# Grouped-query attention, one core: a new order table, first K and Q pieces through SyncE, idle matmuls in the first period

## The chip, the cores and the metric

The kernel runs on one core of a Trainium2 chip. The time is the device time of one execution in microseconds (us); the number that counts is the median of several executions. The engines of the core work on instruction queues of their own: PE (TensorE, matrix multiply, with PEld for the loading of weights), DVE (VectorE), ACT (ScalarE), POOL (GpSimd) and SP (SyncE, which here only issues DMA). They wait for one another through semaphores, and each takes its instructions strictly in the order in which the program puts them.

## The reference

Batch 8, 512 positions, 32 query heads, 8 key/value heads, 64 channels; four query heads share one key/value head.

```python
scores = np.einsum('bhqd,bhkd->bhqk', Q, K_expanded) * scale      # scale = 1/8
weights = np.exp(scores - np.max(scores, axis=-1, keepdims=True))
weights = weights / (np.sum(weights, axis=-1, keepdims=True) + 1e-10)
output = np.einsum('bhqk,bhkd->bhqd', weights, V_expanded)
```

Inputs and output are fp32, with the layout (batch, position, head, channel).

## The kernel before

**Tiles.** The work is cut into pairs of query heads (128 pairs: 8 batches x 16). A pair has four score tiles, one for each block kc of 128 keys: keys on the partitions, two heads x 512 queries along the row, 128x1024 in all. `scores` (L228) fills one with two matmuls of 64 channels, one on each half of the array. The exponential turns the tile into `pt` (fp16), and `pv` (L287) multiplies it by V; V carries a column of ones, so the row sums come out beside the products. `pv` works in chunks: a chunk is one tile and one head, four matmuls (one for each block qc of queries), and a pair has eight chunks. `inverse` (L306) takes the reciprocal of the sums, `norm` (L316) scales the products into `o_sb`, and every fourth pair a 1 MB `store` (L360) goes out through SP. The kernel takes no maximum; it checks at the end that nothing has overflowed and would otherwise run `general_path`.

**Two ways to the exponential.** Of the 32 tiles of eight pairs (a period; there are 16), 27 go to ACT (`exp_act`, L245) and 5 to DVE and POOL. Which 5 is said by `DVE_KCS` (L38): one tuple for each pair of the period, with the kc that DVE takes. Such a tile is scored (D), turned into fp16 bits by DVE (U, L257), its low bits are taken (F, L262), POOL forms a slope and a product (G, L267; W, L275), and DVE adds it to the bits (P, L279). In the first period, tiles of the first two pairs go to ACT all the same, and those of the next two have G and W on DVE too.

**PSUM.** Score tiles for ACT have two buffers (`s_ps`). One region `d_ps` ("a" in the table) and one region `pv` ("b") serve in turn the sums of a pair, a DVE score tile, and the transposes of Q; each is free for its next user when DVE has read it.

**The order.** The order of all instructions is written out by hand in a table: `STEPS` (L39) for each period and `FINISH` (L50) for the last. A token is a letter and a number. S6 refills the score tile for the seventh ACT tile, A6 is its activation; V5.4-6 are chunks 4 and 5 of pair 5 (an a, b or s behind chunk 0 names the region); R and N are inverse and norm; D, U, F, G, W, P are as above, numbered by the DVE tile; T2 transposes the Q of a half unit (four pairs are a unit, half of them g = 0 or 1) on PE, C2 copies it to SBUF on DVE; H reads the check of V; B is a check of the sums; Q0 and Q1 issue on POOL the loads of Q for two periods later and of K (even periods) or V (odd periods) of the next batch. "@1" is work of the period before, "@-1" of the period after. The loop at L501 goes through the periods and skips tokens whose period does not exist, so period 0 has no @1 work.

**K.** For batches 1 to 7, `dma_k` (L175), called at S2 of odd periods, makes the transposed keys by four DMA transposes through SP and two copies, which put the other head of a couple on the other half of the partitions. For batch 0 PE transposes them (`first_k`, L163): once for the couple as it is, once swapped.

**The start.** POOL issues the loads of the first K piece and three Q pieces (with a cast from fp32 to bf16 on the way), builds the identity for the transposes, and goes on with V and the rest. PE does eight idle matmuls on zeros (L496), then transposes K (12 instructions) and the first quarter of Q (L499, L190), DVE copies each, and the first scores follow.

The steps of a period before, in part:

```python
"A0 F4@1 S1 N4@1 V5.4-6@1 G4@1 V5.6-8@1 A1 R5@1 S2 N5@1 D0b W4@1 A2 S3 U0 T1a A3 S4 "
"V6.0-1b@1 H1 V6.1-2@1 C1 V6.2-3@1 A4 P4@1 S5 D1a A5 S6 U1 V6.3-6@1 Q0 V6.6-7@1 Q1 A6 S7 "
```

Of the kernel before, what the change touches and what calls it, by code (L numbers as in the profile page):

```python
# [11 lines left out]
FP32 = mybir.dt.float32  # L12
# [22 lines left out]
VV_HI = 1.0e30  # L35


DVE_KCS = ((), (3,), (), (3,), (3,), (), (3,), (3,))  # L38
STEPS = (  # L39
# [9 lines left out]
).split()  # L49
FINISH = (  # L50
# [10 lines left out]
).split()  # L61


# [19 lines left out]
def fast_path(ctx, tc, Q, K, V, out, flag):  # L83
    nc = tc.nc
# [66 lines left out]
    def d_tile():  # L151
        return d_pool.tile([128, 2, S], FP32, name="d_ps")
# [7 lines left out]
    def region(tok):  # L160
        return {"a": d_tile, "b": pv_tile, "s": s_tile}[tok[-1]]()

    def first_k(gp, swap, bank):  # L163
        half_bank = bank.bitcast(BF16)[:, 0:S]
        ps = half_bank.rearrange("p (sc c) -> p sc c", sc=SC)
        h = 2 * gp
# [6 lines left out]
        return lambda: nc.vector.tensor_copy(out=kt_first[:, gp, swap, :], in_=half_bank)  # L173

    def dma_k(b):  # L175
        kt[b] = kt_pool.tile([128, 2, GP, S], BF16, name="kt")
# [36 lines left out]
    def by_pool(n, k):  # L213
        return n * PPAIR + ON_DVE[k][0] >= UPAIR

    pts, osb, invs, chain, sums, reads, filled, done = ({} for _ in range(8))

    def pt_of(p):
        j = p // NPAIR
# [8 lines left out]
    def scores(p, kc, ps):  # L228
        u, b, gp, g, i = place(p)
        keys = kt_first[:, gp, :, :] if b == 0 else kt[b][:, :, gp, :]  # L230
        for m in range(2):
            nc.tensor.matmul(  # L232
                ps[:, m, :],
                keys[64 * m:64 * m + 64, g ^ m, kc * 128:(kc + 1) * 128],
                qt[u][64 * m:64 * m + 64, g, i, :],
                start=True,
                stop=True,
            )
# [153 lines left out]
    def transposes(j, bank):  # L392
        u, g = divmod(j, 2)
        b, gp = divmod(u, GP)
        todo = reads[j] = []
        if u > 0:
            todo.append(trans_q(u, g, bank[:, 0, :]))
        if b == 0 and gp > 0 and g == 0:
            for swap in range(2):
                todo.append(first_k(gp, swap, bank[:, 1, swap * S // 2:]))  # L400
        if u == NU - 1 and g == 0:
            todo.append(check_v(u, bank[:, 1, S // 2:]))
# [7 lines left out]
    def step(tok, n):  # L410
# [6 lines left out]
        elif what == "A":  # L417
# [3 lines left out]
            if ON_ACT[k + 1:k + 2] == [] or ON_ACT[k + 1][0] != q:  # L421
                for d, (dq, dkc) in enumerate(ON_DVE):
                    if dq == q and not on_dve(n, d):
                        fill(p, dkc)
                        exp_act(p, dkc)
            if n == 0 and k in (0, 2):
                lo, hi, g = ((1, NPAIR, 0), (0, NPAIR, 1))[k // 2]
                trans_q(0, g, d_tile()[:, 0, :], lo, hi)()
            if (n, k) == (0, 4):
                second_loads()  # L430
        elif what in "VRN":
# [6 lines left out]
        elif what in "TCH":  # L438
            j = n * PPAIR // NPAIR + k
            if j < 2:  # L440
                pass
            elif what == "T":
                transposes(j, region(tok))
            else:
                read(j if what == "C" else (j, "v"))
        elif what == "Q":
# [28 lines left out]
                elif what == "P":  # L475
                    exp_join(p, kc)

    load_k(0, 0, 2)
    load_q(0, (0, 2, 4, 8))
    make_identity(nc, ident)  # L480
    nc.gpsimd.memset(ones, 1.0)
    nc.gpsimd.memset(off, 0)
    for j in range(2):
# [7 lines left out]
        load_v(0, gp, gp + 1)  # L491

    nc.vector.memset(warm, 0.0)
    bank = d_tile()
    for j in range(8):
        nc.tensor.matmul(bank[:, 1, :], warm[:, 0:128], warm, start=True, stop=True)  # L496
# [12 lines left out]
def general_path(tc, Q, K, V, out):  # L509
# [114 lines left out]
```

## Time and profile before

| | us |
|---|---|
| median of 3 runs | 420.08 |
| lowest, highest | 419.29, 420.71 |
| the profiled execution | 419.56 |
| its span, first to last instruction | 417.8 |
| busy: ACT, PE, DVE, POOL | 400.3, 384.4, 327.3, 274.4 |
| mean granted clock of PE | 0.978 |
| share of ACT in the chain that ended last | 77% |

The profile is that of one execution. Busy time is the time in which an engine had an instruction under way. The chain that ended last is followed backwards from the last instruction, at each step to whatever released it. Where a timeline merges instructions of one kind, it gives the start of the first, their common length, and how many they are.

### The profile page before, as it was taken

Reading aid. Unit: us, or ns where it says so; the run is one execution under the profiler, and the core shown is the slowest. Engines: PE = TensorE matmul, PEld = TensorE weight load, DVE = VectorE, ACT = ScalarE, POOL = GpSimd, SP = SyncE. Lnnn points to the kernel's source line nnn. Section 1 sums busy time; section 2 is a strip of 40 time slices with the busy share of each in tenths; the row PEclk is TensorE's granted clock in tenths of the full one; section 3 lists DMA queues with packets and bytes.
Section 4 is the critical chain, followed back from the end, with each engine's and each line's share of the span. In section 5 each row is a group of like instructions: output and inputs, shape, how many; then the busy total and the mean of one; then the engine's idle time right before and its main releaser. Section 6 shows DMA issues by size and latency. Waiting matters only on the chain.

```text
span 417.8 us, 13274 instructions
## 1 busy us (share of the span) xinstructions
PE 384.4 (92%) x5817; PEld 240.1 (57%) x5817; DVE 327.3 (78%) x621; ACT 400.3 (96%) x435; POOL 274.4 (66%) x208
## 2 busy tenths in 40 slices
PE   6899899999999999999999999999999999999995
PEld 2355556556556565655656566655655656556563
DVE  1268888797887869888797887879788787978976
ACT  2889999999999999999999999999999999999994
POOL 8316677677676767767676776767667676766660
PEclk9579999999999999999999999999999999999999
DMA  9983996849765895839939489676976599421126
GB/s 101 195 157 122 151 186 153 203 141 174 224 124 150 165 189 205 150 144 176 236 115 235 130 142 195 162 195 141 164 251 117 140 174 204 179 104 56 48 102 207
DMA packets 64078, 66.95 MB, mean 160 GB/s; under 512 B 35088, under 2 KB 38672, under 8 KB 64016
## 3 DMA queue, kind: packets, MB, share of 16 engines
q0 software_dynamic: 29184, 25.17, 41.5%
q1 hardware_dynamic: 34832, 40.90, 33.6%
q8 instruction: 46, 0.75, 0.8%
q14 instruction: 16, 0.13, 0.1%
HBM read 50.33 MB, written 33.55 MB: 201 GB/s over the span
## 4 chain that ended last, share of the span: by engine, by line
ACT 77%; PE 17%; DVE 3%; issue 1%; POOL 1%; ACTq 0%; POOLq 0%
ACT pt L246 77%; PE s_ps L232 9%; PE pv L295 5%; PE d_ps L295 1%; PE d_ps L190 1%; DVE o_sb L322 1%; DVE qt L193 1%; DVE kt_first L173 0%; POOL q_nat L146 0%; PE pv L190 0%; PE d_ps L232 0%; ACTq L246 0%; DVE u L257 0%; PE s_ps L295 0%; POOL k_nat L129 0%
## 5 line engine op out<-in xcount | busy, mean ns | idle before, releaser
L246 ACT ACTIVATE pt<-s_ps 128x1024 f16<-128x1024 f32 x434 | 399.0, 1168 | 11.1 <-PE s_ps L232 11.1
L295 PEld LDWEIGHTS <-pt 128*128 128x128 f16 x4096 | 143.7, 98 | 72.8 <-issue 65.1
L232 PE MATMUL s_ps<-qt,kt 64*128 64x512 bf16 x758 | 148.1, 383 | 19.8 <-ACT pt L246 13.7
L275 POOL TENSOR_TENSOR w<-g,f 128x1024 bf16<-128x1024 bf16 x76 | 161.3, 2123 | 6.3
L267 POOL TENSOR_SCALAR g<-f 128x1024 bf16<-128x1024 int16 x76 | 79.6, 1048 | 121.6 <-DVE f L262 121.6
L295 PE MATMUL pv<-v,pt 128*128 128x65 bf16 x2528 | 118.2, 195 | 1.3 <-DVE kt_first L173 0.6
L232 PEld LDWEIGHTS <-kt 64*128 64x128 bf16 x896 | 50.9, 93 | 68.4 <-issue 37.3
L257 DVE TENSOR_SCALAR u<-d_ps 128x1024 int16<-128x1024 f32 x62 | 75.4, 1216 | 1.3 <-PE d_ps L232 1.3
L295 PE MATMUL d_ps<-v,pt 128*128 128x65 bf16 x1536 | 69.5, 195 | 0.1
L279 DVE TENSOR_TENSOR pt<-u,w 128x1024 uint16<-128x1024 int16 x78 | 53.3, 683 | 8.1 <-POOL w L275 7.9
L322 DVE TENSOR_TENSOR o_sb<-pv,inv 128x512 f32<-128x512 f32 x79 | 54.3, 687 | 1.6
L193 DVE COPY qt<-d_ps 128x1024 bf16<-128x1024 bf16 (+1 forms) x49 | 33.2, 677 | 20.0 <-PE d_ps L201 16.4
L190 PEld LDWEIGHTS <-q_nat 128*128 128x128 bf16 x512 | 29.6, 99 | 12.7 <-issue 8.9
L322 DVE TENSOR_TENSOR o_sb<-d_ps,inv 128x512 f32<-128x512 f32 x48 | 33.2, 691 | 1.6
L262 DVE TENSOR_SCALAR f<-u 128x1024 int16<-128x1024 int16 x78 | 32.4, 416 | 0.0
L190 PE MATMUL d_ps<-ident,q_nat 128*128 128x128 bf16 x384 | 30.2, 222 | 0.9 <-DVE kt_first L173 0.9
L232 PE MATMUL s_ps<-qt,kt_first 64*128 64x512 bf16 x110 | 23.9, 438 | 3.8 <-ACT pt L246 2.8
L193 DVE COPY qt<-pv 128x1024 bf16<-128x1024 bf16 x16 | 11.1, 691 | 20.5 <-PE pv L190 13.8
L311 DVE RECIPROCAL inv<-d_ps 128x8 f32<-128x8 f32 x48 | 9.8, 204 | 20.7 <-PE d_ps L295 20.6
L232 PE MATMUL d_ps<-qt,kt 64*128 64x512 bf16 x108 | 21.1, 383 | 0.0
L311 DVE RECIPROCAL inv<-pv 128x8 f32<-128x8 f32 x79 | 16.1, 204 | 5.7 <-PE pv L295 3.3
L257 DVE TENSOR_SCALAR u<-pv 128x1024 int16<-128x1024 f32 x16 | 19.4, 1215 | 0.5 <-PE pv L232 0.5
(51 smaller groups left out, 116.1 us busy)
## 6 DMA issues: line engine op xcount, KB each, us to landing
out_dram<-o_sb SPq DMA_DIRECT2D x31, 1024.0 KB, 5.4
q_nat<-in_Q_dram POOLq DMA_DIRECT2D x15, 1024.0 KB, 8.9
k_nat<-in_K_dram POOLq DMA_DIRECT2D x7, 512.0 KB, 11.6
v<-in_V_dram POOLq DMA_DIRECT2D x7, 512.0 KB, 13.6
kt<-kt SPq DMA_DIRECT2D x14, 256.0 KB, 5.2
out_dram<-o_sb SPq DMA_DIRECT2D x4, 256.0 KB, 2.4
v<-in_V_dram POOLq DMA_DIRECT2D x4, 128.0 KB, 8.1
q_nat<-in_Q_dram POOLq DMA_DIRECT2D x1, 512.0 KB, 7.5
```

Source lines behind the costliest of these rows:

```text
L190: nc.tensor.transpose(ps[:, i, sc, :], qn[u // 2][:, sc, h:h + 2, :], ident)
L193: return lambda: nc.vector.tensor_copy(out=qt[u][:, g, lo:hi, :], in_=ps[:, lo:hi, :, :].rearrange("p i sc c -> p i (sc c)"))
L232: nc.tensor.matmul(ps[:, m, :], keys[64 * m:64 * m + 64, g ^ m, kc * 128:(kc + 1) * 128], qt[u][64 * m:64 * m + 64, g, i, :], start=True, ...
L246: nc.scalar.activation(out=pt_of(p)[:, kc, :, :], in_=filled.pop((p, kc)), func=EXP, scale=scale)
L257: nc.vector.tensor_scalar(out=st["u"], in0=st["ps"], scalar1=A_U, scalar2=B_U, op0=ALU.mult, op1=ALU.add)
L262: nc.vector.tensor_single_scalar(out=st["f"], in_=st["u"], scalar=1023, op=ALU.bitwise_and)
L267: engine.tensor_scalar(out=g, in0=f, scalar1=-EXP_F1, scalar2=EXP_K * 2.0 ** (24 * (engine is nc.gpsimd)), op0=ALU.add, op1=ALU.mult,)
L275: engine.tensor_tensor(out=w, in0=g, in1=f, op=ALU.mult)
L279: nc.vector.tensor_tensor(out=pt_of(p)[:, kc, :, :].bitcast(U16), in0=st["u"], in1=st["w"], op=ALU.add)
L295: nc.tensor.matmul(sums[p][:, m, qc, :], pt_of(p)[:, kc, m, qc * 128:(qc + 1) * 128], vt[b % 2][:, kc, gp, g * (D + 1):(g + 1) * (D + 1)], ...
L311: nc.vector.reciprocal(out=invs[n][:, k], in_=sums[p][:, :, :, s:s + 1])
L322: nc.vector.tensor_tensor(out=osb[u][:, :, h:h + 2, :].rearrange("p qc m d -> p m qc d"), in0=sums.pop(p)[:, :, :, o:o + D], in1=invs[p // ...
```

## The change

A new table with a new choice of tiles for DVE; the check of V as a token of its own (K) that uses the bank beside the transposes; the first K and Q pieces loaded as fp32 through SP and cast by DVE; the identity ahead of POOL's loads; K of batch 0 transposed one head at a time, put on both halves; and idle matmuls at the start and in period 0, in the place of the V tokens that have no work yet.

```diff
-DVE_KCS = ((), (3,), (), (3,), (3,), (), (3,), (3,))
+DVE_KCS = ((3,), (3,), (), (3,), (), (3,), (3,), ())
 STEPS = (
+    "A0 P4@1 S1 H1 V5.1-3@1 F0 A1 V5.3-5@1 C1 S2 G0 V5.5-7@1 A2 V5.7-8@1 V7.0-1a@1 R5@1 S3 "
+    "W0 N5@1 V7.1-3@1 A3 V7.3-5@1 S4 V7.5-7@1 A4 V7.7-8@1 S5 R7@1 V6.0-1b@1 N7@1 V6.1-2@1 A5 "
+    "V6.2-4@1 S6 P0 V6.4-6@1 A6 V6.6-7@1 F1 V6.7-8@1 S7 R6@1 G1 T2a N6@1 A7 S8 C2 V0.0-1b W1 "
+    "V0.1-2 A8 V0.2-3 S9 D2a V0.3-4 A9 U2 V0.4-5 S10 V0.5-7 A10 V0.7-8 B0@2 S11 P1 V1.0-2a "
+    "A11 V1.2-4 F2 S12 R0 G2 V1.4-5 N0 V1.5-6 A12 V1.6-8 S13 R1 V2.0-1b N1 V2.1-2 W2 A13 "
+    "V2.2-4 S14 D3a A14 U3 S15 V2.4-6 A15 V2.6-8 S16 Q0 R2 T3a N2 A16 S17 P2 V3.0-2b A17 "
+    "V3.2-3 F3 V3.3-4 S18 G3 K3 A18 V3.4-6 H3 C3 S19 V3.6-8 W3 A19 R3 S20 N3 D4a A20 U4 S21 "
+    "T0b@-1 A21 S22 C0@-1 V4.0-2a A22 V4.2-4 P3 S23 D0b@-1 F4 A23 U0@-1 S24 G4 V4.4-6 A24 "
+    "V4.6-8 S25 R4 W4 D1b@-1 N4 A25 S26 U1@-1 Q1 T1a@-1 A26 S0@-1 K1@-1 V5.0-1b "
...
 FINISH = (
...
-    "R5 V4.3-4 N5 V4.4-6 A25 V4.6-7 S26 w3 V4.7-8 V6.0-2a A26 V6.2-3 R4 P3 s4 V6.3-5 N4 a4 "
-    "V6.5-8 V7.0-2s R6 V7.2-4 N6 V7.4-8 R7 N7 B0@2 E1 "
...
+    "W4 V4.6-7 V5.3-4 A24 V4.7-8 V5.4-5 R4 S25 N4 V5.5-7 A25 V5.7-8 S26 V7.0-2a A26 V7.2-3 "
+    "P4 V7.3-5 V6.0-2s R5 V6.2-4 N5 V6.4-5 V7.5-8 V6.5-7 R7 V6.7-8 R6 N7 N6 E1 "
...
+    k_start = const_pool.tile([128, SC, 2, D], FP32, name="k_start")
+    q_start = const_pool.tile([128, SC, 2, D], FP32, name="q_start")
...
-    def first_k(gp, swap, bank):
+    def first_k(gp, g, bank):
...
         for sc in range(SC):
-            if swap:
-                for half, g in ((0, 1), (64, 0)):
-                    nc.tensor.transpose(ps[half:half + 64, sc, :], kn[0][:, sc, h + g, :], ident)
-            else:
-                nc.tensor.transpose(ps[:, sc, :], kn[0][:, sc, h:h + 2, :], ident)
+            for half in (0, 64):
+                nc.tensor.transpose(ps[half:half + 64, sc, :], kn[0][:, sc, 2 * gp + g, :], ident)
...
-            todo.append(trans_q(u, g, bank[:, 0, :]))
+            todo.append(trans_q(u, g, bank[:, 1, :]))
...
         if u > 0 and g == 1:
-            reads[j, "v"] = [check_v(u - 1, bank[:, 1, S // 2:])]
+            banks[j] = bank
+
+    def check_values(j):
+        reads[j, "v"] = [check_v(j // 2 - 1, banks.pop(j)[:, 0, S // 2:])]
...
-            if n == 0 and k in (0, 2):
+            if n == 0 and k in (1, 3):
                 lo, hi, g = ((1, NPAIR, 0), (0, NPAIR, 1))[k // 2]
-                trans_q(0, g, d_tile()[:, 0, :], lo, hi)()
+                bank = d_tile()
+                copies = [trans_q(0, g, bank[:, 1, :], lo, hi)]
+                if g == 1:
+                    copies.append(first_k(0, 1, bank[:, 0, :]))
...
-    load_k(0, 0, 2)
-    load_q(0, (0, 2, 4, 8))
+    def spin(count, columns):
+        bank = pv_tile()
+        for _ in range(count):
+            nc.tensor.matmul(
+                bank[:, 1, 0:columns], warm[:, 0:128], warm[:, 0:columns], start=True, stop=True
+            )
+
+    nc.sync.dma_start(out=k_start, in_=K[0, :, 0:2, :].rearrange("(p sc) g d -> p sc g d", p=128))
+    nc.sync.dma_start(out=q_start, in_=Q[0, :, 0:2, :].rearrange("(sc p) h d -> p sc h d", p=128))
     make_identity(nc, ident)
+    load_q(0, (2, 4, 8))
...
-    for copy in [first_k(0, swap, bank[:, swap, :]) for swap in range(2)]:
-        copy()
-    trans_q(0, 0, d_tile()[:, 0, :], 0, 1)()
+    spin(8, S)
+    nc.vector.tensor_copy(out=kn[0][:, :, 0:2, :], in_=k_start)
+    copy = first_k(0, 0, d_tile()[:, 0, :])
+    copy()
+    nc.vector.tensor_copy(out=qn[0][:, :, 0:2, :], in_=q_start)
+    spin(2, S)
+    copy = trans_q(0, 0, s_tile()[:, 0, :], 0, 1)
+    copy()
+    spin(3, S)
...
+            elif period == 0 and n < 0 and tok[0] == "V":
+                lo, hi = tok[3:].rstrip("abs").split("-")
+                spin(int(hi) - int(lo), S // 2)
```

More of the change, by code (lines that the diff above doesn't have):

```diff
@@ L161, in region @@
         return {"a": d_tile, "b": pv_tile, "s": s_tile}[tok[-1]]()
[L163 removed]
+    def first_k(gp, g, bank):
         half_bank = bank.bitcast(BF16)[:, 0:S]
         ps = half_bank.rearrange("p (sc c) -> p sc c", sc=SC)
[L166 removed]
         for sc in range(SC):
[L168 to L173 removed]
+            for half in (0, 64):
+                nc.tensor.transpose(ps[half:half + 64, sc, :], kn[0][:, sc, 2 * gp + g, :], ident)
+        return lambda: nc.vector.tensor_copy(out=kt_first[:, gp, g, :], in_=half_bank)
     def dma_k(b):
@@ L214, in by_pool @@
         return n * PPAIR + ON_DVE[k][0] >= UPAIR
-    pts, osb, invs, chain, sums, reads, filled, done = ({} for _ in range(8))
+    pts, osb, invs, chain, sums, reads, banks, filled, done = ({} for _ in range(9))
     def pt_of(p):
@@ L396, in transposes @@
         if u > 0:
-            todo.append(trans_q(u, g, bank[:, 0, :]))
+            todo.append(trans_q(u, g, bank[:, 1, :]))
         if b == 0 and gp > 0 and g == 0:
-            for swap in range(2):
-                todo.append(first_k(gp, swap, bank[:, 1, swap * S // 2:]))
+            for side in range(2):
+                todo.append(first_k(gp, side, bank[:, 0, side * S // 2:]))
         if u == NU - 1 and g == 0:
-            todo.append(check_v(u, bank[:, 1, S // 2:]))
+            todo.append(check_v(u, bank[:, 0, S // 2:]))
         if u > 0 and g == 1:
-            reads[j, "v"] = [check_v(u - 1, bank[:, 1, S // 2:])]
+            banks[j] = bank
+    def check_values(j):
+        reads[j, "v"] = [check_v(j // 2 - 1, banks.pop(j)[:, 0, S // 2:])]
     def read(key):
@@ L425, in step @@
                         exp_act(p, dkc)
-            if n == 0 and k in (0, 2):
+            if n == 0 and k in (1, 3):
                 lo, hi, g = ((1, NPAIR, 0), (0, NPAIR, 1))[k // 2]
-                trans_q(0, g, d_tile()[:, 0, :], lo, hi)()
+                bank = d_tile()
+                copies = [trans_q(0, g, bank[:, 1, :], lo, hi)]
+                if g == 1:
+                    copies.append(first_k(0, 1, bank[:, 0, :]))
+                for copy in copies:
+                    copy()
             if (n, k) == (0, 4):
@@ L437, in step @@
                 (inverse if what == "R" else norm)(p)
-        elif what in "TCH":
+        elif what in "TKCH":
             j = n * PPAIR // NPAIR + k
@@ L443, in step @@
                 transposes(j, region(tok))
+            elif what == "K":
+                check_values(j)
             else:
@@ L493, in fast_path @@
     nc.vector.memset(warm, 0.0)
-    bank = d_tile()
-    for j in range(8):
-        nc.tensor.matmul(bank[:, 1, :], warm[:, 0:128], warm, start=True, stop=True)
-    for copy in [first_k(0, swap, bank[:, swap, :]) for swap in range(2)]:
-        copy()
-    trans_q(0, 0, d_tile()[:, 0, :], 0, 1)()
+    spin(8, S)
[5 more added lines that the diff above has]
+    copy = trans_q(0, 0, s_tile()[:, 0, :], 0, 1)
+    copy()
+    spin(3, S)
     for period in range(-2, NPER):
```

2 lines of the change are left out of this document (1 added, 1 removed), and 25 rows, old and new, of tables (FINISH, STEPS).

## The prediction

> **What bounds the kernel now.** I read the page's busy times first, then what ScalarE (ACT) waited for, then its timeline, then windows of the clock. All times are us.
>
> ```profile
> PE 384.4 (92%) x5817; PEld 240.1 (57%) x5817; DVE 327.3 (78%) x621; ACT 400.3 (96%) x435; POOL 274.4 (66%) x208
> ```
>
> ```profile
> ACT pt L246 <- PE s_ps L232: 11.1, 11, 6.5
> ```
>
> ACT is the fullest engine, and the only thing it ever waits for is a refilled score tile: eleven times, 6.5 of the 11.1 before its first activation. Its timeline says where (start, length, what, in brackets the idle time before):
>
> ```profile
> 8.69 2.85 ACT L246 ACTIVATE pt<-s_ps 128x1024 f16<-128x1024 f32 x3 [6.53 <-PE s_ps L232]
> ...
> 20.64 1.94 ACT L246 ACTIVATE pt<-s_ps 128x1024 f16<-128x1024 f32 x2 [1.38 <-PE s_ps L232]
> ...
> 23.17 1.02 ACT L246 ACTIVATE pt<-s_ps 128x1024 f16<-128x1024 f32 x1 [0.59 <-PE s_ps L232]
> 24.48 1.02 ACT L246 ACTIVATE pt<-s_ps 128x1024 f16<-128x1024 f32 x1 [0.29 <-PE s_ps L232]
> 25.79 1.02 ACT L246 ACTIVATE pt<-s_ps 128x1024 f16<-128x1024 f32 x1 [0.29 <-PE s_ps L232]
> 27.35 7.44 ACT L246 ACTIVATE pt<-s_ps 128x1024 f16<-128x1024 f32 x8 [0.54 <-PE s_ps L232]
> ...
> 48.77 1.94 ACT L246 ACTIVATE pt<-s_ps 128x1024 f16<-128x1024 f32 x2 [0.45 <-PE s_ps L232]
> 50.99 361.27 ACT L246 ACTIVATE pt<-s_ps 128x1024 f16<-128x1024 f32 x394 [0.28 <-PE s_ps L232]
> ```
>
> After 51 there is no gap until ACT ends at 412.26. Windows (busy PE, PEld, DVE, ACT, POOL, then granted clock, DMA) show why the early part has gaps and the rest none:
>
> ```profile
> 6.51:9.92 3.41, 1.58 (x14) 0.85 (x14) 1.56 (x4) 1.23 (x2) 3.41 (x6) 1.00 1.33 139
> 9.92:13.33 3.41, 2.72 (x18) 1.20 (x17) 0.84 (x2) 3.13 (x4) 3.21 (x9) 0.50 1.22 181
> 16.75:20.16 3.41, 3.11 (x26) 1.83 (x25) 0.06 (x1) 2.51 (x3) 0.00 (x0) 0.50 1.15 211
> 23.57:26.99 3.42, 3.42 (x44) 2.27 (x41) 2.17 (x4) 2.67 (x3) 0.00 (x0) 0.50 1.12 216
> 26.99:30.40 3.41, 3.41 (x60) 2.33 (x60) 1.23 (x3) 3.05 (x4) 1.13 (x2) 1.00 0.49 96
> ...
> 89.32:114.07 24.75, 23.18 (x365) 14.69 (x363) 20.25 (x40) 24.75 (x28) 17.74 (x12) 1.00 0.95 193
> ```
>
> After a 3.41 stretch with PE busy 1.58 (46%) the clock falls to half. A stretch at 91% does not raise it, one at 100% does. A settled period is 24.75 = 27 activations of 0.917, ACT full. So the span is a sum: first activation 8.69 + 434 x 0.917 = 397.8 + the ten later gaps 4.54 + about 0.1 for each of 11 runs (one alone lasts 1.02, in a run 0.917) + 5.55 after the last activation = 417.7 (the page: 417.8). Execution is 419.56, so 1.75 lies around the span; the median of the runs, 420.08, is 0.52 above this execution. A change can only move the 8.69, the 4.54 + 1.1, the 5.55, or break the settled periods.
>
> **The first activation.** Before, POOL issues K and three Q loads (1.41 to 4.63) and only then builds the identity, ready at 5.23; the transposes begin at 5.27. After, `make_identity` comes first (0.27 + 0.29, done near 2) and K and Q come through SP. No load by SP is in the trace. Nearest rows: a 256 KB store by SP lands in 2.4, a 256 KB copy inside SBUF in 5.2, POOL's 128 KB K load in 3.3. I take 2.5 (same queue and size as the store). From about 1.0, where the other engines start, that is 3.5; the cast (128x512, rows from 0.42 for a copy to 0.69 for an fp32 product) ends by 4.1. The eight 512-column matmuls hold PE from 1.33 to 4.75 anyway, as before, so K is hidden up to a landing of 3.1, and at 5.2 everything is 1.1 later. Then: 8 half transposes 0.64 (row at 5.79) to 5.4; kt copy 0.42 to 5.87; cast of Q behind it on DVE to 6.25; 4 transposes 0.38; copy 0.42 to 7.15; scores 0.42: first activation 7.65. The two idle matmuls (0.85 at half speed) lie beside kt copy and cast. The three behind the Q transposes cost 0.65 at full speed, beside the copy, but 1.28 at half speed, then 8.3. Before, one more transpose set (0.59), one more copy (0.34) and the wait for the identity lay on this path. I take 7.9: gain 0.8, bounds 1.05 and -0.1.
>
> **The early gaps.** The 23 idle matmuls of 256 columns fill the places of the pv chunks that period 0 does not have (V5, V7, V6 with @1). At full speed one is 0.11 (half of 0.22), a refill 0.32, so PE is busy 0.6 to 0.85 of each 0.917, above the 71% (2.41 of 3.40, from 48.0 to 51.4) that kept the full clock in this trace. They delay a refill only when the clock is low: 0.21 each, 0.4 to 0.9 a step, and then PE is at 100% and rises within a stretch or two; I allow 0.4. That removes the gaps from 11.83 to 27.35 (3.37 + six runs 0.6). What stays: the first batch's K transposes, 8+8+8 in one step (before 8+4+8; rows 0.46, 0.31, 0.35, now about 1.16 for 1.12), twice at full speed before: 0.44 with two runs and 0.73 with two, so 0.65 and 0.93. Now four places have it: 16 transposes at A3 (0.87 + refill 0.32 + two idle 0.22 = 1.4 against 0.917 and a slack of about 0.3): 0.15; T2a, T0b, T2a: 0.4 each; and the one DVE-only chain of period 0 (0.37 + 0.37 + 0.6 + 0.6 ahead of N0): 0.4. Sum with the 0.4: 2.2, bounds 1.2 and 4. Before 5.64: gain 3.4.
>
> **The settled periods.** Still 27 activations and 5 tiles on DVE and POOL. On PE no step holds more than a refill and four chunks of 4, which the trace has at the pace: refill at 69.48, 16 matmuls, next refill at 70.40, 0.92. I laid one period out by row spacings (u 1.13, join or copy 0.60, f 0.37, inverse and norm 0.85, POOL 1.13 + 2.07, S(k+1) at the start of A(k)). Every region is free before PE reaches its next user. Tightest: N0 done at 11.15 and V2.0-1b at 11.32; N1 12.0 and D3a 12.24; U2 9.23 and V1.0-2a 9.49; at the boundary P4 waits for W4, and C1 behind it ends at 1.25 of the next period for V7.0-1a at 1.64. PE may be late by another 0.4 (refill ends 0.31 to 0.46 before it is due: the 0.31 PE waits for ACT). So 0. If one chain is longer by x above 0.57, each of 14 periods loses x - 0.57.
>
> **Q1 moves to the end of the period, behind W4 on POOL.** K (even periods) and V (odd) now start near 24.26: U4 ends 19.35, C0 19.95, P3 20.55, F4 20.9, G4 from 21.06, W4 from 22.19, then the load 2.07 later. V is first read by V0.0-1b at 24.75 + 6.42 + 0.37 = 31.54, 7.3 after the issue (before it was some 31). V has no lone row: behind Q it landed 4.0 to 8.0 after Q did; with Q's own start of about 1.5 and 0.33 more issue that is 5.8 to 9.8; the first 128 KB piece landed in 3.2, with 384 KB more at 180 GB/s 5.3. I take 5.8, because Q is now issued 10 earlier and has landed. A price by the Trainium skill, DMA: Bandwidth & Descriptors, section "Anatomy of one DMA — SWDGE (gpsimd) path": 2.0 plus the bytes at 436 GB/s, an estimate of 3.2 for V; by that it would have 4 to spare; the trace's 5.3 and more disagrees. K lands near 4.5 of the odd period; SP's four transposes took 10 to 16.7 until the copies were issued, beside stores and loads that now come later; at 10 and 5.2 for the copies kt is ready at 20.2, D0b reads it at 20.5. SP's stores wait behind it, some 8 later; three o_sb buffers cover that. Price 0, thin.
>
> **The end.** Activations stay 434 (one more in period 0, one less in FINISH). Before, R7 started 0.59 after the last activation and N7 ended 1.88 after it. After, the last PE work is V7.6-8, V6.5-7, V6.7-8; so R7, R6, checks 0.37, N7 and N6: about 0.45 + 0.4 + 0.24 + 0.37 + 0.6 + 0.69 = 2.75. Loss 0.85, bounds 0.3 and 1.2; the last store (2.4) follows both times.
>
> **Sum.** 419.56 - 0.8 - 3.4 + 0.85 = 416.2, on the median of the runs 416.7.
>
> **Rivals.**
> (1) *V lands late.* From 7.7 after its issue (7.3 + 0.4) PE stops at V0.0-1b, and S9 and ACT behind it, at all seven batch changes: 7 x (landing - 7.7). From 8.2 it eats the gain. At the 9.8 bound: 416.7 + 14.7 = 431; at 8.5: 422.3. For: that landing occurred behind Q with transposes beside. Against: neither is now beside it. K late to D0b is priced alike. 0.10.
> (2) *A handover is too tight*, each period loses 0.3: 14 x 0.3 = 4.2, 420.9. For: margins of 0.17 to 0.26 on laid-out sums. Against: PE's 0.4, and the old table had DVE waiting 0.57 for POOL each period with ACT full. 0.12.
> (3) *The clock falls in period 0 all the same*, where T2a's 24 transposes stand (1.2 of a 3.41 stretch). The gaps from 20 to 27 return, 2.5 to 3.5: 419.7. For: the 6.51 stretch that fell had 0.8 of its 1.58 in transposes; the 16.75 stretch at 91%, 20 of its 26 matmuls transposes, did not rise. Against: the other steps are far fuller. 0.13. The Trainium skill, TensorE: Matmul & The Clock Gate, section "Part 4: PE-mode transpose", says that transposes don't count as PE-busy in the same way; those two stretches agree, and by it this rival is likelier than the busy shares make it.
> (4) *The idle matmuls don't do what they say*, PE is slow at the start and the first activation stays at 8.7: 417.5, inside my range.
>
> **How the numbers follow.** Forecast 0.60 with (4) 0.05 in it, (1) 0.10, (2) 0.12, (3) 0.13, better than forecast (first activation 7.65, gaps 1.2, end +0.3: 414.8) 0.05. Likeliest time 416.7, its own range 415 to 418.6. The range 414.8 to 422 leaves out most of (1) and some of (2). 0.3% (1.26) is what a measurement can tell: faster is below 418.8: 0.60 + 0.05 + part of (2) and (3), 0.70; slower above 421.3: (1), half of (2) and a little of (3), 0.17; same 0.13.
>
> **What would show it.** First activation 7.6 to 8.4; no ACT gap of 0.5 or more before 30, granted clock 1.00 throughout from 10 on; settled periods 24.75 (in windows of 24.75, ACT 24.75); the last activation ends 2.7 before the last norm. A PE wait for V by DMA at the batch changes proves (1), for a DVE norm in every period (2), a 0.50 clock in the windows (3). A settled period longer by 0.25 makes the prediction wrong.

## The result, and the profile after

| | before | after |
|---|---|---|
| median, us (4 runs each, same chip) | 419.69 | 430.28 |
| lowest to highest | 418.17 to 420.71 | 429.08 to 431.77 |
| the profiled execution | 419.56 | 429.47 |
| its span | 417.8 | 427.4 |
| mean granted clock | 0.978 | 0.989 |

The ratio is 1.0257, 95% interval [1.0207, 1.0307]: the changed kernel is 10.6 slower, where 3.4 faster was forecast. The busy times of the changed kernel (the page):

```profile
PE 383.8 (90%) x5861; PEld 242.5 (57%) x5861; DVE 334.7 (78%) x621; ACT 401.6 (94%) x435; POOL 276.9 (65%) x208
```

ACT has as much to do as before (400.3), so the time is idle time of ACT. Its own wait is again only for refills; what PE, which makes them, newly waits for stands in the second line (total, times, longest):

```profile
ACT pt L244 <- PE s_ps L230: 17.0, 16, 5.4
...
PE pv L293 <- DMA v<-in_V_dram: 9.3, 5, 4.1
```

The timeline of ACT (start, length, instructions, idle time before) shows where:

```profile
7.54 4.69 ACT L244 ACTIVATE pt<-s_ps 128x1024 f16<-128x1024 f32 x5 [5.38 <-PE s_ps L230]
12.64 4.81 ACT L244 ACTIVATE pt<-s_ps 128x1024 f16<-128x1024 f32 x5 [0.41 <-PE s_ps L230]
17.87 1.94 ACT L244 ACTIVATE pt<-s_ps 128x1024 f16<-128x1024 f32 x2 [0.42 <-PE s_ps L230]
20.06 3.77 ACT L244 ACTIVATE pt<-s_ps 128x1024 f16<-128x1024 f32 x4 [0.25 <-PE s_ps L230]
24.93 12.36 ACT L244 ACTIVATE pt<-s_ps 128x1024 f16<-128x1024 f32 x13 [1.10 <-PE s_ps L230]
...
47.53 73.47 ACT L244 ACTIVATE pt<-s_ps 128x1024 f16<-128x1024 f32 x80 [0.25 <-PE s_ps L230]
121.71 49.60 ACT L244 ACTIVATE pt<-s_ps 128x1024 f16<-128x1024 f32 x54 [0.72 <-PE s_ps L230]
171.68 49.60 ACT L244 ACTIVATE pt<-s_ps 128x1024 f16<-128x1024 f32 x54 [0.36 <-PE s_ps L230]
222.06 49.60 ACT L244 ACTIVATE pt<-s_ps 128x1024 f16<-128x1024 f32 x54 [0.78 <-PE s_ps L230]
275.80 1.02 ACT L244 ACTIVATE pt<-s_ps 128x1024 f16<-128x1024 f32 x1 [4.13 <-PE s_ps L230]
277.31 98.39 ACT L244 ACTIVATE pt<-s_ps 128x1024 f16<-128x1024 f32 x107 [0.50 <-PE s_ps L230]
377.09 1.02 ACT L244 ACTIVATE pt<-s_ps 128x1024 f16<-128x1024 f32 x1 [1.38 <-PE s_ps L230]
```

From 121 on gaps come at distances of about 50 or 100: 54 activations are two periods, so they stand at the change from one batch to the next. With the two behind 377 (0.50, 0.29) they are 8.66, and each of eight restarts costs another 0.1: 9.5 in all. A period without such a gap keeps its pace, all 24.75 of it filled by ACT (busy PE, PEld, DVE, ACT, POOL, then clock and DMA):

```profile
338.00:362.75 24.75, 23.13 (x366) 14.90 (x363) 20.82 (x40) 24.75 (x29) 17.14 (x12) 1.00 0.72 165
```

The difference of the two profiled executions, 9.91, is made of:

| | us |
|---|---|
| first activation, 8.69 to 7.54 | -1.15 |
| gaps at the batch changes | +9.5 |
| the rest between first and last activation (403.57 to 412.14, less the 9.5) | -0.9 |
| from the last activation to the end of the span, 5.54 to 7.72 | +2.2 |
| around the span, 1.75 to 2.07 | +0.3 |

The -0.9 is itself a difference: -1.4 up to 52, and +0.5 in waits at the batch changes that are too short for the timeline to list (it merges activations less than 0.15 apart). With those, V's lateness costs 10.0.

One batch change, the longest, on three queues. First SP's timeline of the changed kernel, then POOL's loads in the same stretch, then PE:

```profile
244.14 6.04 SPq L176 DMA_TRANSPOSE kt<-k_nat  x4
251.55 1.11 SPq L181 DMA_DIRECT2D kt<-kt  x2
252.78 34.34 SPq L361 DMA_DIRECT2D out_dram<-o_sb  x4
```

```profile
252.27 0.82 POOL L148 DMA_DIRECT2D q_nat<-in_Q_dram  x1
262.95 1.23 POOL L137 DMA_DIRECT2D v<-in_V_dram  x1
```

```profile
274.41 0.80 PE L293 MATMUL pv<-v,pt 128*128 128x65 bf16 x12 [4.13 <-DMA v<-in_V_dram]
```

V is issued at 262.95. PE comes to V0.0-1b at 274.41 - 4.13 = 270.28, 7.3 later, exactly where the prediction had it, and V is there 4.1 later still. The five late loads land 8.41, 8.06, 8.47, 11.33 and 9.06 after their issue; less 7.7 (the lead, and the 0.4 that PE may be late by the prediction) that is 0.71, 0.36, 0.77, 3.63 and 1.36, and ACT's gaps are 0.72, 0.36, 0.78, 4.13 and 1.38. SP's wait list names the step in front of it:

```profile
SPq L176 <- DMA k_nat<-in_K_dram: 77.7, 7, 11.9
```

Seven times SP stands at the transposes, about 11 each, until K has landed; the stores behind them in its queue leave only when K's copies are out, here at 252.78, half a microsecond after POOL has issued Q. The median Q load (the page's DMA part: KB each, us to landing) now takes 12.8, before 8.9; the seven of the odd periods, which go ahead of V, take 11.3 to 15.3, and V is issued 10.4 to 10.7 behind them, so none of the seven has landed by then:

```profile
q_nat<-in_Q_dram POOLq DMA_DIRECT2D x15, 1024.0 KB, 12.8
...
v<-in_V_dram POOLq DMA_DIRECT2D x7, 512.0 KB, 8.4
```

### The profile page after: what moved, and what is told of

Same layout as the page of the kernel before. It is cut to its first block, busy times and chain, and to the rows that moved or that the text cites. A ratio compares the mean times of both kernels' runs of the same rounds, so it can differ in the third digit from the quotient of the medians.

```text
span 427.4 us, 13375 instructions
## 1 busy us (share of the span) xinstructions
PE 383.8 (90%) x5861; PEld 242.5 (57%) x5861; DVE 334.7 (78%) x621; ACT 401.6 (94%) x435; POOL 276.9 (65%) x208
## 4 chain that ended last, share of the span: by engine, by line
ACT 41%; PE 33%; DMA 11%; DVE 7%; POOL 4%; issue 2%; ACTq 0%
ACT pt L244 41%; PE s_ps L230 13%; DMA v<-in_V_dram 11%; PE pv L293 9%; PE d_ps L293 5%; POOL w L273 3%; PE d_ps L188 2%; PE pv L489 2%; DVE u L255 2%; POOL g L265 1%; DVE o_sb L320 1%; DVE pt L277 1%; DVE qt L191 1%; PE d_ps L230 1%; DVE f L260 1%
## 5 line engine op out<-in xcount | busy, mean ns | idle before, releaser
L244 ACT ACTIVATE pt<-s_ps 128x1024 f16<-128x1024 f32 x434 | 400.3, 1220 | 17.2 <-PE s_ps L230 17.0
L273 POOL TENSOR_TENSOR w<-g,f 128x1024 bf16<-128x1024 bf16 x77 | 163.7, 2127 | 6.4
L265 POOL TENSOR_SCALAR g<-f 128x1024 bf16<-128x1024 int16 x77 | 80.8, 1050 | 133.2 <-DVE f L260 133.1
L293 PE MATMUL pv<-v,pt 128*128 128x65 bf16 x2528 | 114.7, 196 | 11.0 <-DMA v<-in_V_dram 9.3
L255 DVE TENSOR_SCALAR u<-d_ps 128x1024 int16<-128x1024 f32 x48 | 58.6, 1221 | 29.9 <-PE d_ps L230 29.9
L293 PE MATMUL d_ps<-v,pt 128*128 128x65 bf16 x1536 | 67.2, 194 | 0.1
L188 PEld LDWEIGHTS <-q_nat 128*128 128x128 bf16 x512 | 29.1, 98 | 15.4 <-issue 10.6
L255 DVE TENSOR_SCALAR u<-pv 128x1024 int16<-128x1024 f32 x30 | 36.5, 1216 | 0.0
L230 PE MATMUL s_ps<-qt,kt_first 64*128 64x512 bf16 x112 | 21.7, 384 | 2.0 <-ACT pt L244 1.6
L230 PE MATMUL d_ps<-qt,kt 64*128 64x512 bf16 x84 | 16.8, 388 | 0.0
L200 DVE TENSOR_REDUCE okv<-d_ps 128x1 f32<-128x128 f32 x31 | 8.9, 288 | 9.4 <-PE d_ps L199 9.4
## 6 DMA issues: line engine op xcount, KB each, us to landing
q_nat<-in_Q_dram POOLq DMA_DIRECT2D x15, 1024.0 KB, 12.8
```

What stands on the lines that cost most here:

```text
L230: nc.tensor.matmul(ps[:, m, :], keys[64 * m:64 * m + 64, g if b == 0 else g ^ m, kc * 128:(kc + 1) * 128], qt[u][64 * m:64 * m + 64, g, i, :],
L244: nc.scalar.activation(out=pt_of(p)[:, kc, :, :], in_=filled.pop((p, kc)), func=EXP, scale=scale)
L255: nc.vector.tensor_scalar(out=st["u"], in0=st["ps"], scalar1=A_U, scalar2=B_U, op0=ALU.mult, op1=ALU.add)
L265: engine.tensor_scalar(out=g, in0=f, scalar1=-EXP_F1, scalar2=EXP_K * 2.0 ** (24 * (engine is nc.gpsimd)), op0=ALU.add, op1=ALU.mult,)
L273: engine.tensor_tensor(out=w, in0=g, in1=f, op=ALU.mult)
L293: nc.tensor.matmul(sums[p][:, m, qc, :], pt_of(p)[:, kc, m, qc * 128:(qc + 1) * 128], vt[b % 2][:, kc, gp, g * (D + 1):(g + 1) * (D + 1)], ...
```

## The experiments

The theory that the runs were to test (called V1 in the expectations): K, issued at the end of an even period, reaches SP's transposes late; SP's queue is strictly in order, so a store due earlier is held behind K's copies and goes out together with POOL's loads of Q and V; those stretch, and V, which now has a lead of only 7.3, comes too late. The median of the kernel before was 419.25 on the chip of the first eight runs, 418.94 for the next three and 418.86 for the last one.

### Q1 back beside Q0

```diff
-    "V2.2-4 S14 D3a A14 U3 S15 V2.4-6 A15 V2.6-8 S16 Q0 R2 T3a N2 A16 S17 P2 V3.0-2b A17 "
+    "V2.2-4 S14 D3a A14 U3 S15 V2.4-6 A15 V2.6-8 S16 Q0 Q1 R2 T3a N2 A16 S17 P2 V3.0-2b A17 "
...
-    "V4.6-8 S25 R4 W4 D1b@-1 N4 A25 S26 U1@-1 Q1 T1a@-1 A26 S0@-1 K1@-1 V5.0-1b "
+    "V4.6-8 S25 R4 W4 D1b@-1 N4 A25 S26 U1@-1 T1a@-1 A26 S0@-1 K1@-1 V5.0-1b "
```

> The changed kernel with Q1 put right behind Q0 (behind S16), so that K and V are both issued some 10 us earlier in the period; nothing else. Theory V (the time was lost by PE waiting for a V that was issued 7.3 us before its first use): the five waits for V, 9.3 us, and the 9.5 us that ACT lost by them are gone; 430.3 - 9.5 = 420.8, range 419.5 to 422, no PE wait for V. Rival T (the new order is too tight by itself, and V is only what PE happens to stand at): 426 or more.

Measured: 419.95, ratio 1.0012 [1.0002, 1.0023]. No wait for V is left, and ACT runs to its end without a gap that the timeline lists:

```profile
48.09 362.19 ACT L244 ACTIVATE pt<-s_ps 128x1024 f16<-128x1024 f32 x395 [0.25 <-PE s_ps L230]
```

So the place of Q1 is all of the loss. With it undone the change is worth nothing, though, not the 3.4 of the forecast: the other terms were off too (below).

### One of the two loads at a time

K beside Q0, V left at the end of the period:

```diff
-        if k == 1 and b + 1 < B:
+        if k == odd and b + 1 < B:
             (load_v if odd else load_k)(b + 1)
```

V beside Q0 (behind Q), K left at the end:

```diff
-        if k == 1 and b + 1 < B:
+        if k == 1 - odd and b + 1 < B:
             (load_v if odd else load_k)(b + 1)
```

> The changed kernel with only the loads of K (even periods) moved to Q0; V stays at the end of the odd periods. Theory V1 (V is pushed: K lands late, SP's four transposes and two copies hold the stores back, the stores collide with the load of Q, and V queues behind Q): with K early the stores leave on time, V lands in about 7 us instead of a median of 8.4, waits for V fall below 2 us in total: 420.5 to 422.5. Theory V2 (the lead of 7.3 is too short whatever else moves): at least 5 us of waits for V stay, 426 to 430.

> The changed kernel with only the loads of V (odd periods) moved to Q0; K stays at the end of the even periods. Theories V1 and V2 both: no wait for V, 420.8 like the run with both early. If K at the end of the period costs something of its own (kt late for D0b in the period after), this is slower than the run with both early by the PE waits at the tiles scored with kt: my sum has kt 0.3 us ahead of D0b, so 0 to 3 us.

Measured: 420.21, ratio 1.0026 [1.0014, 1.0037], with K early; 430.71, ratio 1.0295 [1.0247, 1.0343], with V early.

The second expectation failed outright, and that is the most useful result of the study: V issued some 9.8 earlier in the period is late all the same, and V left at the end of the period is in time if only K is early. V's own short lead is therefore not enough as a cause, and not needed either; between these kernels it is the place of K that decides. With K early, SP's timeline of the same stretch is (first start 244.14 in the changed kernel):

```profile
238.96 5.13 SPq L176 DMA_TRANSPOSE kt<-k_nat  x4
245.47 1.11 SPq L181 DMA_DIRECT2D kt<-kt  x2
246.70 33.23 SPq L361 DMA_DIRECT2D out_dram<-o_sb  x4
```

SP waits for K at its transposes here too, six times:

```profile
SPq L176 <- DMA k_nat<-in_K_dram: 43.9, 6, 8.5
```

But against Q's issue in the odd period K has landed earlier, 11.2 to 13.0 ahead of it, where the changed kernel has 8.2 to 9.5. So the first store leaves at 246.70, 3.4 ahead of Q's issue (250.12), and V, issued at 260.78, takes 6.9 (median of the seven):

```profile
v<-in_V_dram POOLq DMA_DIRECT2D x7, 512.0 KB, 6.9
```

With V early and K late, V stands behind the stretched Q in POOL's queue, and PE waits for it at every batch change:

```profile
PE pv L293 <- DMA v<-in_V_dram: 10.4, 7, 3.1
```

Its V takes 18.2 from issue to landing (the page's DMA part, median of the seven):

```profile
v<-in_V_dram POOLq DMA_DIRECT2D x7, 512.0 KB, 18.2
```

### K's chain on SP behind the stores

```diff
-            if k == 2 and n % 2 == 1 and n // 2 + 1 < B:
+            if k == 8 and n % 2 == 1 and n // 2 + 1 < B:
                 dma_k(n // 2 + 1)
```

> The changed kernel, Q1 still at the end of the period, with one edit: the K work that SP does for the next batch (four DMA transposes and two copies) is called six steps later, at S8 of the odd periods, so that SP's two stores of that stretch stand ahead of it in SP's queue instead of behind it. Theory V1 (the K load issued at the end of an even period lands after SP has come to its transposes; SP holds there, the stores behind it go out late and all at once, and the loads of Q and V of that period, which POOL has under way then, land late): the stores leave on their own dates, V lands within 8 of its issue in nearly all periods, PE's wait for V falls from 18 in all to under 3, and the time is 419.5 to 422. Rival V3 (the transposes of K or the K load disturb Q and V wherever they lie): V still lands 10 or more after issue in some periods, PE waits for it 6 or more in all, time 425 to 431.

Measured: 454.75, ratio 1.0849 [1.0814, 1.0884], outside both expectations. The wait for V is gone, as the theory said, and another one stands in its place:

```profile
PE pv L230 <- DMA kt<-kt: 26.6, 7, 4.3
```

The transposes now start at 99.64 of a period whose D0b wants the result at about 114, the copies are issued at 110.03, and seven times ACT stands for 2.9 to 4.2, then for 0.26 to 0.52 twice more. K's chain has no room to move back by six steps. For the question it was made for the run says little: V lands 7.0 to 8.7 after its issue, but every odd period is longer than in the changed kernel, so V is also due later. That K's chain is as close to its due time as V is what it shows.

### A store held back, K early

```diff
+        elif done[u] == UPAIR and u % 2 and u // 4 + 1 < B and u % 4 == 1:
+            held.append(u)
...
+    def release(p, kc):
+        while held:
+            nc.sync.dma_start(out=bell, in_=pt_of(p)[0:1, kc, 0, 0:2])
+            store(held.pop(), 0, 2 * HPG)
...
+            if k == 16:
+                release(p, kc)
```

> The kernel with only the loads of K moved beside Q0 (420.21 in its run, V still issued at the end of the odd periods, no wait for V), and one thing added: in the odd periods 1 to 13 the store that is due at N6@1 (about 13 into the period) is held back on SP until the activation A16 (about 15.5 to 16.5), by a copy of four bytes of that activation's result ahead of it in SP's queue. So the store goes out beside Q0's load, as in the changed kernel, but K's loads, transposes and copies stay early. Theory V1 (a store held back into Q's load stretches it, and V, behind Q on POOL's queue, lands late): Q takes 10 or more to land in the odd periods, V lands 8 or more after its issue in several, PE waits for V 4 or more in all, time 423 to 430. Rival V4 (it takes K's own transposes and copies beside Q as well; one held store alone is too little): V lands within 7.5, PE does not wait for it, time 420 to 421.

This is the kernel with K early; one store of each batch is kept back until A16. Measured: 428.82, the median of 427.08, 428.00, 429.64 and 433.89; the ratio, 1.0222 [1.0197, 1.0246], goes by the three shorter ones, and the profile is that of the longest, so the size of its waits is not theirs. K's transposes and copies are nearly as early as in the run above; one store alone is held, by a copy of four bytes ahead of it in SP's queue, and goes out 1.9 ahead of the next one (its timeline, the same batch change). PE's wait for V is back (its waits, then the page's DMA part):

```profile
245.72 6.09 SPq L176 DMA_TRANSPOSE kt<-k_nat  x4
253.19 2.30 SPq L181 DMA_DIRECT2D kt<-kt  x2
261.07 0.63 SPq L339 DMA_DIRECT2D bell<-pt  x1
261.82 15.39 SPq L371 DMA_DIRECT2D out_dram<-o_sb  x3
```

```profile
PE pv L293 <- DMA v<-in_V_dram: 11.7, 7, 2.3
```

```profile
v<-in_V_dram POOLq DMA_DIRECT2D x7, 512.0 KB, 9.2
```

So a late store is enough, with nothing wrong at K. One part of the expectation did not hold: Q of the odd periods takes 9.6 to 10.8, no longer than with K early (8.7 to 11.8). Q has landed when V is issued, 0.4 to 1.1 before in six of the seven and 0.2 behind in the one shown, and V still takes 8.0 to 9.5, against 6.6 to 7.6 with K early. So V is stretched by the late store itself, and not only through Q. The packets of V at this batch change take 6.1 (272.3 to 278.4) against 4.0 (262.7 to 266.7) with K early, and start 2.6 after the issue against 1.9. Packets of stores move beside the first 1.4 of these 6.1 and the last 0.7; what holds V up in between is not shown.

### V ahead of Q

```diff
-        if k == 0 and n + 2 < NPER:
+        if k == odd and n + 2 < NPER:
             load_q(n + 2)
-        if k == 1 and b + 1 < B:
+        if k == 1 - odd and b + 1 < B:
             (load_v if odd else load_k)(b + 1)
```

> The changed kernel with one edit: in the odd periods POOL issues V at Q0's place and Q at Q1's place, at the end of the period (before: the other way round). K stays at the end of the even periods, so SP's queue still holds the stores back until K's copies are out, and they still go out beside what POOL loads then. Theory V1's last step (V is late because its packets stand behind those of the stretched Q load on POOL's queue, not because V's own are slow): with V ahead of Q, V lands within 15 of an issue that is 10 earlier, no wait for V is left; Q, 10 later, is wanted only some 20 later: 419.5 to 421.5. Rival: whatever is loaded beside the late stores is stretched as far, V too (it has pieces of 256 bytes): V lands 17 or more after its issue as in the run with V moved behind Q0, PE waits for it 5 or more in all, 424 to 430.

Measured: 418.80 (418.22 to 420.79), ratio 0.9995 [0.9985, 1.0004], a little below the range expected. SP holds its stores as in the changed kernel (its timeline), but V is issued at 252.42 and Q at 263.09:

```profile
244.33 6.05 SPq L176 DMA_TRANSPOSE kt<-k_nat  x4
251.76 1.11 SPq L181 DMA_DIRECT2D kt<-kt  x2
252.99 29.24 SPq L361 DMA_DIRECT2D out_dram<-o_sb  x4
```

```profile
v<-in_V_dram POOLq DMA_DIRECT2D x7, 512.0 KB, 11.7
```

V still takes 11.7, since it is now the load that lies beside the stores; that much the rival had right. But it has 10.7 more to do it in, and Q, which is wanted some 20 later, follows. In the run with V early V is issued at the same place of the period, but right behind Q, and takes 18.2; here Q comes 10.7 later and V takes 11.7. So 6.5 of V's time there goes with Q in front of it. In the profiled execution, the longest of eleven, PE waits once, 1.39, for the copies of kt, with gaps of ACT of 0.84 at 160.7 and 0.53 at 164.4: the other short lead, K's, is still there.

### What the idle matmuls of period 0 do

```diff
-            elif period == 0 and n < 0 and tok[0] == "V":
-                lo, hi = tok[3:].rstrip("abs").split("-")
-                spin(int(hi) - int(lo), S // 2)
```

> The kernel with Q1 beside Q0 (419.95 in its run) without the 23 idle matmuls that fill the empty V places of period 0; the idle matmuls of the start (8, 2, 3) stay. Theory C (the idle matmuls hold the clock in period 0): without them a 3.41 stretch with PE near half busy comes, the granted clock falls to 0.50 before 20, ACT waits for refills by about 2 more than the 2.95 in all, time 421 to 423. Rival D (the start alone, with its thirteen idle matmuls and K transposes by halves, carries the clock over; the idle matmuls only take places on PE): the clock stays 1.00, the gaps stay or shrink, time 418.5 to 420.2.

Measured, from the kernel with Q1 beside Q0: 419.84, ratio 1.0014 [0.9998, 1.0030]; with them 1.0012. Half of each expectation holds. The clock does fall, for one stretch of 3.41 (two windows of this kernel, then one of the changed kernel; the column before the last two is the clock, and the second and the third window hold the transposes of T2a):

```profile
12.54:15.95 3.41, 1.71 (x12) 0.59 (x12) 0.71 (x3) 3.41 (x5) 0.39 (x1) 1.00 1.63 191
15.95:19.36 3.41, 3.41 (x42) 2.23 (x39) 1.35 (x3) 2.28 (x3) 0.00 (x0) 0.50 1.13 213
```

```profile
15.05:18.46 3.41, 3.30 (x48) 1.90 (x46) 0.91 (x2) 2.99 (x4) 0.00 (x0) 1.00 1.37 207
```

The fall follows a window in which PE is busy 1.71, 0.20 of it in transposes; it ends after one that PE fills, 1.67 of it with transposes. But up to 21 the fall costs gaps of 1.00 and 0.29, where with the idle matmuls 0.41, 0.42 and 0.25 stand: they keep the clock, and take on PE about as much as the clock would.

### The chain that DVE does alone, and the old table

```diff
             elif what == "F":
                 exp_low(st)
-                if not by_pool(n, k):
-                    slope(nc.vector, st["f"], st["g"])
-                    bend(nc.vector, st["f"], st["g"], st["w"])
-                    exp_join(p, kc)
-            elif by_pool(n, k):
-                engine = nc.gpsimd if what in "GW" else nc.vector
+            else:
+                engine = nc.gpsimd if what in "GW" and by_pool(n, k) else nc.vector
```

> The kernel with Q1 beside Q0 (419.95 in its run) with one edit in period 0: the one chain that DVE does alone there (F, G, W, P of tile 2, issued in one piece at F2) is issued at its own places in the table, so that N0 and the reads of PSUM do not stand behind 1.9 of DVE work. Theory: the gap of 1.09 at 24.9, whose cause is V2.0-1b waiting 1.2 for N0, falls to 0.3 or less and nothing replaces it: 418.9 to 419.5. Rival: the pieces delay R0, R1 and the next score tile instead, the gap moves a few steps on: 419.7 to 420.5.

Measured: 418.79, ratio 0.9988 [0.9973, 1.0003], against 1.0012 with the chain in one piece. The gap of 1.09 is gone and none came for it; 17 activations run through where it was:

```profile
20.45 16.02 ACT L244 ACTIVATE pt<-s_ps 128x1024 f16<-128x1024 f32 x17 [0.25 <-PE s_ps L230]
```

The next two kernels take the table and the choice of tiles of the kernel before, with the new start and the idle matmuls; the second leaves out the idle matmuls for V7:

```diff
-            elif period == 0 and n < 0 and tok[0] == "V":
+            elif period == 0 and n < 0 and tok[0] == "V" and tok[1] != "7":
```

> The old table (STEPS, FINISH, DVE_KCS, the check of V inside the transposes) under the new start: first K and Q through SyncE and cast, identity first, batch 0's K one head at a time, idle matmuls at the start and in period 0 (20 of 256 columns). Theory: first activation 7.5 (1.15 earlier), clock kept in period 0, so the early gaps lose another 1 to 3; the end as before. 419.7 - 1.15 - 1 to 3 = 415.5 to 417.6. Rival (idle matmuls without the new table put refills off as much as the clock brings): 419 or more.

> The old order table with the new start and idle matmuls (418.89 in its run), without the idle matmuls that stand for V7 tokens in period 0: the first of them came behind T2b and waited 1.5 for DVE to read K's transposes out of the same region, with a gap of ACT of 2.21 at 21. Theory: the gap falls to 0.4 to 1.0, the clock stays up because the later steps have pv work, time 417.2 to 418.0, below the kernel before. Rival: without those eight the clock falls and the gaps of the kernel before come back in part: 418.7 to 420.

Measured: 418.89, ratio 0.9995 [0.9983, 1.0006], and 417.50, ratio 0.9958 [0.9940, 0.9975]. The first missed its range: an idle matmul stood behind T2b in the same region of PSUM and waited 1.5 until DVE had read K out of it. Without it the gap falls from 2.21 to 1.14 (timelines of the two):

```profile
20.96 12.02 ACT L244 ACTIVATE pt<-s_ps 128x1024 f16<-128x1024 f32 x13 [2.21 <-PE s_ps L230]
```

```profile
19.65 4.76 ACT L244 ACTIVATE pt<-s_ps 128x1024 f16<-128x1024 f32 x5 [1.14 <-PE s_ps L230]
```

The gap stayed a little wider than expected (0.4 to 1.0), the time was in its range. What the expectation says of the clock did not hold: it fell to half for one stretch here, which the kernel with all the idle matmuls does not have:

```profile
17.09:20.51 3.42, 2.95 (x30) 1.67 (x28) 1.40 (x4) 2.28 (x3) 0.00 (x0) 0.50 1.14 216
```

So the old table with the new start is faster than both kernels, by 0.42% against the one before.

### POOL's closing

In nearly all kernels with the new start the end after the flag is longer. The trace's records of POOL after the branch on the flag (start, instruction, duration in ns), before and after:

```
415.656 INC_SWDGE_SEM 397      424.254 INC_SWDGE_SEM 608
416.084 DRAIN 894              424.893 DRAIN 1711
```

```diff
-    load_q(0, (8, 16))
-    load_k(0, 4, KV)
+    load_q(0, (8, 12, 16))
+    load_k(0, 4, 6)
+    load_k(0, 6, KV)
```

> The old table with the new start and fewer idle matmuls (417.50 in its run), with two of POOL's first loads cut in two, so that POOL issues 40 loads in all, as the kernel before does, in place of 38. In every kernel with the new start POOL's closing takes longer than in the kernel before: its last drain 1.71 against 0.89 and the semaphore step ahead of it 0.61 against 0.40. Theory: that hangs on the number of POOL's loads; with 40 both are short again, the end after the flag is 1.0 shorter, time 416.3 to 416.9. Rival: it hangs on something else in the new start (the two loads by SP), both stay long, time 417.3 to 418.

> The changed kernel with Q1 beside Q0 and the chain of period 0 in pieces (418.79 in its run), with POOL's loads cut so that they are 40, and in the last period the last chunks of pair 6 ahead of those of pair 7, with R6 N6 before R7 N7. Theory: 1.0 from POOL's closing if it hangs on the number of loads, 0.3 to 0.5 from the tail, because N6 then runs beside the last activation: 417.2 to 417.7. Rival: neither counts, 418.5 to 419.

In both the drain is 0.894 again and the step ahead of it 0.397. The second kernel also has `V6.4-8 R6 N6 V7.5-8 R7 N7` at its end. Measured: 417.38, ratio 0.9958 [0.9943, 0.9973], against 0.9958 without the two cuts; and 417.65, ratio 0.9970 [0.9959, 0.9981], against 0.9988. The traces of these two behave as the theory said, but the theory falls by another kernel: the one with V ahead of Q issues 38 loads too, and its drain takes 731. So it is not the number. Nor is the gain shown in the time: the first pair shows no difference, the second 0.75 (0.0018 of 419), with the tail's order in it. Each drain is that of one execution, and the profiled execution of the kernel with 417.50 was 418.33, so whether its drain is as long in the others is not shown either.

## Why the prediction was wrong

**The step that failed** is the paragraph on Q1 with its "Price 0, thin". It had the mechanism in two halves and priced both at nothing. "SP's stores wait behind it, some 8 later; three o_sb buffers cover that" asked only who waits for the stores, and not what they then run into: POOL's loads. "I take 5.8, because Q is now issued 10 earlier and has landed" is the size that went wrong by it, and its reason was false at all seven batch changes: Q landed 0.9 to 4.6 after V's issue. With the stores on time V takes 6.9 (the run with K early), already over 5.8 but inside the due time of 7.3; beside the late stores the median is 8.4 and the worst 11.3. The due time was right to a tenth. The Trainium skill's price for it (DMA: Bandwidth & Descriptors, "Anatomy of one DMA — SWDGE (gpsimd) path"), from which the estimate of 3.2 was worked out, is further off: the quickest run has a median of 6.9.

Rival (1) had the place, the sign that would prove it and the price: 422 to 431 at a landing of 8.5 to 9.8, and its rule, landing less 7.7, gave four of the five gaps to 0.02 (the longest has 0.5 more, with PE at half its clock behind the stall). Its chance of 0.10 was too low for the same reason: its "against" was that neither Q nor transposes lie beside V any more, and the stores were not on that list. What it did not have is the cause. V's short lead alone brings no wait (420.21 with K early); here it took K's late landing, SP's order, and the stores. With that lead a held store suffices (ratio 1.0222 [1.0197, 1.0246]); with V ahead of Q and the longer lead the held stores do no harm (0.9995).

**The early gaps** were a mis-sized term: gain 3.4 forecast, 0.9 in the changed kernel's execution, 1.4 without V's short waits. In the kernel with Q1 beside Q0, which has no wait for V, the stretch from the first to the last activation is 402.16 (8.12 to 410.28) against 403.57. The clock behaved as forecast, 1.00 from the first activation to the end of period 0, and rival (3) did not come: the stretch 15.05 to 18.46, which holds the 24 transposes of T2a, kept 1.00 beside the idle matmuls, and so did the next. By the rule of the Trainium skill that the prediction cites (TensorE: Matmul & The Clock Gate, "Part 4: PE-mode transpose") the fall was likelier. The run without the idle matmuls speaks against that rule: the clock fell there behind idle time with 0.20 of transposes, and it came back behind a stretch of which transposes fill 1.67. The stretch of 16.75 in the kernel before, which the prediction cites for it, stays as it is; what sets the two apart is open. But the gaps no longer hung on the clock. The chain that DVE does alone cost 1.1 where 0.4 was put down, and the places with K's transposes 0.41, 0.42, 0.25 and three small ones (0.21, 0.31, 0.25). These seven sum to 2.95; with 0.1 for each restart and some shorter waits, 4.2 stayed where 2.2 was put down.

**The end** was mis-sized as well: 0.85 forecast, 2.2 measured. The part that was worked out, the second norm behind the last activation, is right: the last norm ends 2.78 after it, before 1.88, so 0.9. The rest is what was taken to be the same: POOL's last drain (1.71 for 0.89) and the step ahead of it (0.61 for 0.40), together 1.0, and 0.3 between the last norm and that step, where the flag is read and loaded.

**The first activation** was near, but not to be had so exactly: 7.9 forecast, 7.54 measured here (a gain of 1.15, over the bound of 1.05), 7.55 with K early and 7.93 to 8.12 in the other kernels with this table. The K load by SP takes 3.1 (2.5 was put down, and up to 3.1 it was to be hidden). What makes the difference of 0.4 to 0.6 is not shown; K has landed at 3.97 in a kernel with 7.55 and in one with 7.93. **The settled periods** cost nothing, as forecast: 24.75. Rival (2), a handover too tight, did not come.

Of the miss of 13.6 (430.28 against 416.7) V is 10.0, the early gaps 2.0, the end 1.3, what lies around the span 0.3; the first activation gave back 0.35. The last 0.3 is the distance of the median from the profiled execution, 0.8 where 0.5 was taken.

## What to carry to other kernels

When a load is moved on an in-order queue, follow everything behind it to where it will then land, not only to who waits for it: a store that nobody needs can still slow the one load that somebody does. A lead that is just long enough by rows from the old schedule is too short if the move itself makes the load slower; give the short lead to the transfer whose user is furthest away (here Q rather than V). And when a trick has removed a cause of gaps, cost what is left at those places anew: the next limit there is rarely zero.

## What the runs showed of the hardware

A 512 KB load by POOL in pieces of 256 bytes takes 6.6 to 7.6 where the 1 MB store by SP ahead of it lands 0.7 to 2.9 after its issue (K early), and 7.1 to 11.3 where the stores land 3.7 to 8.5 after it (changed kernel); there it lands 2.8 to 4.1 behind the last of these stores. With the stores and K's copies beside it from the start it takes 10.2 to 15.3 (V ahead of Q). Q's 1 MB load goes from a median of 9.0 (K early) to 12.8 (changed kernel), and the stores' own from 6.2 to 6.8.

PE's stall for V has an echo. In the changed kernel PE does nothing from 270.80 to 274.20, and the next stretch has a mean clock of 0.54 although PE is busy 3.19 of its 3.40 (windows):

```profile
270.80:274.20 3.40, 0.00 (x0) 0.00 (x0) 0.00 (x0) 0.87 (x1) 1.53 (x1) 1.00 1.02 311
274.20:277.60 3.40, 3.19 (x34) 1.76 (x35) 1.38 (x3) 1.31 (x2) 0.00 (x0) 0.54 0.06 24
277.60:281.00 3.40, 3.40 (x67) 2.41 (x65) 2.62 (x6) 3.35 (x4) 2.31 (x2) 0.96 0.02 5
```

The gap of 4.13 is followed by one of 0.50 for that reason: a refill takes 0.61 there, not 0.39.

POOL's closing drain takes 894 ns in the kernel before and in the two with the loads cut (40 loads by POOL), 731 in the kernel with V ahead of Q (38 loads), and 1711 in the changed kernel and the nine others with 38. What sets it stays open.
